# Down projection, output blocks 0 to 7: all 22 k pairs by seven products in two passes, and the FFN norm's factor moved onto the up projection's input

## The chip, the cores and the metric

One Trainium2 chip, one of its cores. The metric is device time in microseconds of one execution of the whole kernel. Engines are named as in the profile: PE is TensorE's matmuls, PEld its weight loads, DVE is VectorE, ACT ScalarE, POOL GpSimd, SP the engine that issues most DMAs.

## The reference

One layer of a bidirectional encoder with 256 tokens and 2048 channels in float32: a mixer (attention and a state space branch), then a gated feed-forward part with a convolution over tokens, then a final RMSNorm. The change touches the feed-forward part:

```python
def conv_ffn(h, w_up, conv_w, conv_b, w_down):
    u = centred_dwconv(h @ w_up, conv_w, conv_b)
    gate, val = jnp.split(u, 2, axis=-1)
    return (jax.nn.silu(gate) * val) @ w_down
...
    h = h + conv_ffn(rms_norm(h, norm_ffn_w[l]), ffn_w_up[l], ffn_conv_w[l], ffn_conv_b[l],
                     ffn_w_down[l])
return rms_norm(h, norm_final_w)
```

`w_up` has 2048 rows and 2 x 5632 columns, `w_down` 5632 rows and 2048 columns, and the convolution takes three tokens. In blocks of 128: 16 channel blocks, 44 gate and 44 value blocks, 16 output blocks.

## The kernel before, in words

**Numbers in two parts.** Every float32 operand of a product is split into a high part (a copy on ScalarE into a rounded type, `wh`) and a low part (what is left, a subtraction on VectorE, `wl`), by `hilo` (L149) or in `split_to` (L205). A product is three matmuls: high by high, high by low, low by high. Weights come in by DMA on SP's queue into three raw buffers (`RAWB=3`, `load`, L119) and are split in halves of eight 128x128 blocks into five buffers for each part (`HB=5`), so splits run up to five halves ahead of TensorE, and a raw buffer is loaded again once the job in it is split.

**Jobs.** The program is a list of jobs, each with a weight source, a function that issues its matmuls by half, an evacuation, and side functions (`at`, L1309) that run just ahead of it. A `dense` job (L235) multiplies 16 (or 14) blocks of weights with the activations. Its high parts go first (L252, one matmul of 512 columns per block, which gives high and low of the input side by side), then its low parts (L259, one of 256). Jobs marked `mate` go by twos: high of both, then low of both (main loop, L1589 on). With `late` set, the last so many blocks of both high parts are put behind the rest (`high`, L1552).

**Up projection.** For each of 44 up pairs m there is one gate and one value job. Their input is `hHL`, the residual stream times the norm's weight, made by `wo_evac` (L1066) before the norm's factor r_ffn is known; `ffn_r` (L1082) makes r_ffn at the end of the first up job. `conv3` (L1088) therefore multiplies the job's result by r_ffn (`sum_times`, L304: a copy on ScalarE, an addition in L302 and a multiplication in L309 on VectorE), then convolves (L1091, L1093). `gate_ev` and `val_ev` make the activation `aHL[kp]`, where k pair kp holds the blocks 2kp and 2kp+1.

**Down projection, output blocks 0 to 7.** Eight output blocks and one k pair make a 2x2 product of block matrices: two halves of 128 tokens by two k blocks, and two k blocks by two groups of four output blocks. Products of 128 tokens with 512 columns accumulate in PSUM over the k pairs. For k pairs 0 to 17 (`sevens`, L1122) it is done with seven products in place of eight, from sums of activations (`act_sums`, L1124, names W1, R, N4, N2) and sums of weights. Four of the seven (M1, M5, M7, M6) are the first pass, `unit_one` (L1152), which runs between up pairs: one behind every even m from 2 to 36. It splits the raw weights B11 and three sums of weights (`split_one`, L178), and stores three things in DRAM for later: the sum T2 (`t2D`), the activation sum N4 (`n4D`), and for kp below 14 the activation itself (`aD`). The other three (M2, M3, M4) are the second pass, `second` (L1170, `split_two` L195), which loads two quarters of the weights, T2, and by `n4_load` and `a_load` N4 and the activation. Three second units stand behind up pairs 38, 40 and 42; the rest come after the up projection. k pairs 18 to 21 are `plain` (L1183): eight products into M2, M3, M4 and a fourth sum P22. `inner` (L1194) takes the first four sums out of PSUM when k pair 17 is done, `last_unit` (L1205) the other four when all is done; `seven_channels` (L1219) turns the result back to channels during block 12.

**Output blocks 8 to 15** are dense jobs: `d8` to `d15` for k blocks 28 to 43, and `e8` to `e15` for k blocks 0 to 27, whose activations `a_load` brings back. The order after the up projection is written by hand in L1482 to L1484 (`p` plain, `s` second, `d` and `e` as above), and by which job each reload is put ahead of (L1480, L1499).

**Buffers and order.** Activations, sums and reloads share 29 page buffers; TensorE's sums use eight PSUM banks, four for dense jobs and four for M1 to M7 and small things. Engines take their instructions in order; that order is made ahead of time from the program's order and dependencies. SP issues the loads, the stores and the reloads from one queue.

## Time and profile before

| what | us |
|---|---|
| runs before | 1935.64, 1936.91, 1933.70 (median 1935.64) |
| the profiled execution | 1935.64 |
| its span | 1933.1 |
| TensorE busy | 1919.3 |
| VectorE busy | 1610.6 |
| ScalarE busy | 1274.1 |
| up projection, with the down units in it | about 1197 to 1744 |
| rest of the down projection | about 1744 to 1920 |

The page of the profile gives the busy time of each engine and the costliest groups of instructions; a group's row reads: line, engine, operation, output <- inputs with shapes, count, then busy time and mean duration, then the engine's idle time just ahead of them and what ended it. Matmul durations there overlap, so that a matmul's price is read from how many follow each other in a stretch.

### The profile page before, as it was taken

Reading aid. Unit: us, or ns where it says so; the run is one execution under the profiler, and the core shown is the slowest. Engines: PE = TensorE matmul, PEld = TensorE weight load, DVE = VectorE, ACT = ScalarE, POOL = GpSimd, SP = SyncE. Lnnn points to the kernel's source line nnn. Section 1 sums busy time; section 2 is a strip of 40 time slices with the busy share of each in tenths; the row PEclk is TensorE's granted clock in tenths of the full one; section 3 lists DMA queues with packets and bytes.
Section 4 is the critical chain, followed back from the end, with each engine's and each line's share of the span. In section 5 each row is a group of like instructions: output and inputs, shape, how many; then the busy total and the mean of one; then the engine's idle time right before and its main releaser. Section 6 shows DMA issues by size and latency. Waiting matters only on the chain.

```text
span 1933.1 us, 28910 instructions
## 1 busy us (share of the span) xinstructions
PE 1919.3 (99%) x10812; PEld 1678.0 (87%) x10812; DVE 1610.6 (83%) x2690; ACT 1274.1 (66%) x2048; POOL 16.2 (1%) x36
## 2 busy tenths in 40 slices
...
GB/s 284 207 155 145 170 131 229 275 220 173 218 223 172 216 231 169 211 239 162 173 196 202 216 250 175 228 254 245 255 239 237 250 243 229 227 214 337 272 261 112
DMA packets 170859, 417.82 MB, mean 216 GB/s; under 512 B 10720, under 2 KB 108192, under 8 KB 143840
## 3 DMA queue, kind: packets, MB, share of 16 engines
...
q0 software_dynamic: 1024, 1.54, 0.3%
...
## 4 chain that ended last, share of the span: by engine, by line
PE 92%; DVE 3%; ACT 2%; DMA 2%; issue 1%; SPq 0%; DVEq 0%; ACTq 0%
PE g L252 36%; PE g L259 19%; PE g L977 11%; PE s L1143 5%; PE g L287 3%; PE g L288 3%; PE g L289 3%; PE s L977 2%; PE g L231 1%; PE g L233 1%; PE g L232 1%; DVE wl L226 1%; PE s L252 1%; PE s L882 1%; PE s L891 1%
## 5 line engine op out<-in xcount | busy, mean ns | idle before, releaser
L226 DVE TENSOR_TENSOR wl<-raw,wh 128x1024 fp32r<-128x1024 f32 x598 | 716.0, 1212 | 164.9 <-ACT wh L225 89.6
L225 ACT ACTIVATE wh<-raw 128x1024 fp32r<-128x1024 f32 x598 | 620.2, 1049 | 275.3 <-PE g L252 80.7
L252 PE MATMUL g<-xHL,wh 128*128 128x512 f32 x1424 | 341.7, 392 | 0.2 <-DVE cu L302 0.2
L252 PE MATMUL g<-hHL,wh 128*128 128x512 f32 x1408 | 327.2, 390 | 0.0
L252 PEld LDWEIGHTS g<-hHL,wh 128*128 128x128 f32 x1408 | 262.8, 188 | 53.5
L252 PEld LDWEIGHTS g<-xHL,wh 128*128 128x128 f32 x1424 | 262.5, 188 | 52.1 <-PE s L233 0.4
L259 PEld LDWEIGHTS g<-xHL,wl 128*128 128x128 f32 x1424 | 182.6, 191 | 6.9
L259 PE MATMUL g<-xHL,wl 128*128 128x256 f32 x1424 | 184.7, 283 | 0.0
L259 PEld LDWEIGHTS g<-hHL,wl 128*128 128x128 f32 x1408 | 174.8, 192 | 3.4
L259 PE MATMUL g<-hHL,wl 128*128 128x256 f32 x1408 | 176.0, 283 | 0.0
L150 ACT ACTIVATE wh<-raw 128x1024 fp32r<-128x1024 f32 (+1 forms) x118 | 87.0, 752 | 83.6 <-DMA raw<-in_w_dn 30.3
L977 PE MATMUL g<-wh,yHL 128*128 128x512 f32 x392 | 125.0, 390 | 0.0
L151 DVE TENSOR_TENSOR wl<-raw,wh 128x1024 fp32r<-128x1024 f32 (+1 forms) x118 | 96.6, 839 | 11.2 <-PE g L259 5.9
L1093 DVE SCALAR_TENSOR_TENSOR uc<-u,V,uc 128x255 f32<-128x255 f32 x176 | 84.3, 479 | 20.6 <-ACT uc L1091 18.4
L287 PE MATMUL g<-wh,xHL 128*128 128x512 f32 x256 | 100.4, 392 | 0.0
L288 PE MATMUL g<-wl,xHL 128*128 128x512 f32 x256 | 100.0, 390 | 0.0
L289 PE MATMUL g<-wh,xHL 128*128 128x512 f32 x256 | 99.8, 390 | 0.0
L1091 ACT ACTIVATE uc<-u,V 128x256 f32<-128x256 f32 x88 | 52.0, 591 | 62.3 <-DVE u L309 62.3
L977 PEld LDWEIGHTS g<-wh,yHL 128*128 128x128 f32 x392 | 73.6, 188 | 15.2
L252 PE MATMUL g<-aHL,wh 128*128 128x512 f32 x338 | 78.9, 390 | 0.0
L977 PE MATMUL g<-wl,yHL 128*128 128x512 f32 x196 | 76.3, 389 | 0.0
L252 PEld LDWEIGHTS g<-aHL,wh 128*128 128x128 f32 x338 | 63.2, 188 | 13.1
...
## 6 DMA issues: line engine op xcount, KB each, us to landing
...
raw<-in_w_in SPq DMA_DIRECT2D x128, 256.0 KB, 3.9
...
FB<-acsD SPq DMA_DIRECT2D x32, 512.0 KB, 7.3
...
```

The source lines that it names most:

```text
L150: act.activation(wh, v, AF.Copy)
L151: dve.tensor_sub(wl, v, f32(wh))
L225: act.activation(vh, r, AF.Copy)
L226: dve.tensor_sub(vl, r, f32(vh))
L252: pe.matmul(ps, lhsT=wh[:, b, :], rhs=x, start=k == 0, stop=False)
L259: pe.matmul(cell["ps"][:, 0, :], lhsT=wl[:, b, :], rhs=get(k)[:, 0, :], start=False, stop=k == ktot - 1)
L287: pe.matmul(ps, lhsT=x[:, 0, ts], rhs=wH[:, kk, :], start=k == 0, stop=False)
L288: pe.matmul(ps, lhsT=x[:, 0, ts], rhs=wL[:, kk, :], start=False, stop=False)
L289: pe.matmul(ps, lhsT=x[:, 1, ts], rhs=wH[:, kk, :], start=False, stop=k == kt - 1)
L977: pe.matmul(M[nm], lhsT=x, rhs=w, start=left[nm] == total[nm], stop=left[nm] == 1)
L1093: dve.scalar_tensor_tensor(o[:, a], u[:, b], vcol("fcw", k * 88 + cb), o[:, a], ALU.mult, ALU.add)
L1143: pe.matmul(M[nm], lhsT=x, rhs=w, start=left[nm] == total[nm], stop=left[nm] == 1)
```

## The change

- The sets of products change. First pass: M5, M7, M6, M4, from the sums W1, R, N2 and the activation A22 and from four sums of weights (T13 with two, T24 with two), so that `split_one` makes four sums and splits two halves of 1024 columns. Second pass: M1, M2 and M3 from three of the four weight quarters as loaded, without a sum: `split_two` has no addition, and its source is 512 KB and 256 KB of `w_dn`. T2 is no longer stored or loaded.
- All 22 k pairs go this way; `plain` and P22 are gone. `inner` works on M5, M6, M7, M4 when the last first unit is done, `last_unit` on M1, M2, M3.
- First units 0 to 20 stand behind up pairs 5, 7, 9, 11, 13, 15, 17, 18, 20, 22, 24, 26, 28, 30, 31, 33, 35, 37, 39, 41 and 42; unit 21 behind `d9`. No second unit stands in the up projection. The order after it begins with `d8 d9`, and `d8` has `late = 2`.
- `rescale` makes the input again with the factor in it: for each of the eight pairs of channel blocks two operations of VectorE (residual times weight times r_ffn), a high and a low, put ahead of jobs of up pairs 1 to 5. From up pair 6 on the jobs read it, and `conv3` no longer multiplies.
- N4 is reloaded in six groups at other places, activations from `u21` on.

```diff
@@ -132,7 +132,7 @@
             for h in range(2):
                 nc.sync.dma_start(t[:, 8 * h:8 * h + 8, :], j.src[:, 8 * h:8 * h + 8, :])
         elif j.seven == 2:
-            nc.sync.dma_start(t[:, :8, :], j.src[0])
+            nc.sync.dma_start(t[:, :8, :].rearrange("p (m k) c -> p m (k c)", m=4), j.src[0])
             nc.sync.dma_start(t[:, 8:12, :], j.src[1])
         elif j.wide:
             nc.sync.dma_start(t.rearrange("p (m k) c -> p m (k c)", m=8), j.src)
@@ -179,28 +179,23 @@
 
 
         r = raws[i].rearrange("p (m k) c -> p m k c", m=8)
-        B11, B12, B22 = r[:, :4, 0, :], r[:, 4:, 0, :], r[:, 4:, 1, :]
+        B11, B12, B21, B22 = r[:, :4, 0, :], r[:, 4:, 0, :], r[:, :4, 1, :], r[:, 4:, 1, :]
         if h == 0:
-            t, t2 = page([P, 2, 4, P], name="T13"), page([P, 4, P], name="T2")
-            sums[i], T2[jobs[i].kp] = t, t2
+            t, u = sums[i] = page([P, 2, 4, P], name="T13"), page([P, 2, 4, P], name="T24")
             dve.tensor_add(t[:, 0], B11, B12)
             dve.tensor_add(t[:, 1], B22, B12)
-            hilo(wh[:, :4, :], wl[:, :4, :], B11)
-            hilo(wh[:, 4:, :], wl[:, 4:, :], t[:, 0])
-            dve.tensor_add(t2, t[:, 0], B22)
+            hilo(wh, wl, t.rearrange("p t m c -> p (t m) c"))
+            dve.tensor_add(u[:, 0], t[:, 0], B22)
+            dve.tensor_add(u[:, 1], u[:, 0], B21)
         else:
-            hilo(wh[:, :4, :], wl[:, :4, :], sums.pop(i)[:, 1])
-            hilo(wh[:, 4:, :], wl[:, 4:, :], T2[jobs[i].kp])
+            hilo(wh, wl, sums.pop(i)[1].rearrange("p t m c -> p (t m) c"))
 
     def split_two(i, h, wh, wl):
-        r = raws[i]
         if h == 0:
-            dve.tensor_add(r[:, 8:12, :], r[:, 8:12, :], r[:, 0:4, :])
-            hilo(wh, wl, r[:, 0:8, :])
+            vh, vl = (w.rearrange("p (k m) c -> p m k c", k=2) for w in (wh, wl))
+            hilo(vh, vl, raws[i][:, :8, :].rearrange("p (m k) c -> p m k c", m=4))
         else:
-            hilo(wh[:, :4, :], wl[:, :4, :], r[:, 8:12, :])
-
-    T2 = {}
+            hilo(wh[:, :4, :], wl[:, :4, :], raws[i][:, 8:12, :])
 
     def split_to(n):
         while hptr[0] < min(n, len(halves)):
@@ -300,13 +295,6 @@
     def halves_sum(ps, o):
         act.activation(o, ps[:, 1, :], AF.Copy)
         dve.tensor_add(o, o, ps[:, 0, :])
-
-    def sum_times(ps, r, o):
-        if len(ps.shape) == 2:
-            dve.tensor_mul(o, ps, r)
-        else:
-            halves_sum(ps, o)
-            dve.tensor_mul(o, o, r)
 
     def token_sums(accs):
 
@@ -1083,11 +1071,25 @@
         r_ffn["r"] = rsqrt_of([ssh], D, "r_ffn")
 
 
+    TURNED = 6
+    nF = {}
+
+    def rescale(j):
+        v = page([P, 2, S], name="nF")
+        t = nF[j] = page([P, 2, 2, S], F32R, name="hHL")
+        for b in range(2):
+            m = 2 * j + b
+            dve.scalar_tensor_tensor(v[:, b, :], hp[m // 4][:, m % 4, :], vcol("nffn", m), r_ffn["r"], ALU.mult,
+                                     ALU.mult)
+        hilo(t[:, 0], t[:, 1], v)
+
     gv, aHL = {}, {}
 
     def conv3(ps, cb):
         u, o = p1(name="u"), p1(name="uc")
-        sum_times(ps, r_ffn["r"], u)
+        halves_sum(ps, u)
+        if cb % NFF < TURNED:
+            dve.tensor_mul(u, u, r_ffn["r"])
         act.activation(o, u, AF.Identity, scale=vcol("fcw", 88 + cb), bias=vcol("fcb", cb))
         for k, a, b in ((0, slice(1, S), slice(0, S - 1)), (2, slice(0, S - 1), slice(1, S))):
             dve.scalar_tensor_tensor(o[:, a], u[:, b], vcol("fcw", k * 88 + cb), o[:, a], ALU.mult, ALU.add)
@@ -1111,15 +1113,14 @@
             dve.tensor_sub(lo, o, f32(hi))
             if m % 2 == 0:
                 even[0] = o
-            elif m // 2 in sevens:
+            else:
                 act_sums(aS, m // 2, even[0], o)
         return ev
 
 
 
     even, aS = {}, {}
-    NS, NK = 18, 22
-    sevens = set(range(NS))
+    NK = 22
 
     def act_sums(st, kp, e, o):
         w = page([P, 4, P], name="asum")
@@ -1130,17 +1131,15 @@
 
     aD = dr.tile([NK, P, 2, 2, S], F32, name="aD")
     n4D = dr.tile([NK, P, 2, P], F32, name="n4D")
-    t2D = dr.tile([NK, P, 4, P], F32, name="t2D")
     n4, M, tok, left = {}, {}, {}, {}
-    for nm in ("M1", "M5", "M7", "M6", "M2", "M3", "M4", "P22"):
-        left[nm] = (3 * NS if nm != "P22" else 0) + (6 * (NK - NS) if nm in ("M2", "M3", "M4", "P22") else 0)
-    total = dict(left)
+    for nm in ("M5", "M7", "M6", "M4", "M1", "M2", "M3"):
+        left[nm] = 3 * NK
 
     def add(nm, aH, aL, bH, bL):
         if nm not in M:
             M[nm] = spsum([P, 512])
         for x, w in ((aH, bH), (aH, bL), (aL, bH)):
-            pe.matmul(M[nm], lhsT=x, rhs=w, start=left[nm] == total[nm], stop=left[nm] == 1)
+            pe.matmul(M[nm], lhsT=x, rhs=w, start=left[nm] == 3 * NK, stop=left[nm] == 1)
             left[nm] -= 1
 
     def half(w, a):
@@ -1151,62 +1150,54 @@
 
     def unit_one(kp, spill):
         def mm(h, n, wh, wl):
-            for a, (nm, lf) in enumerate(((("M1", "A11"), ("M5", "W1")), (("M7", "R"), ("M6", "N2")))[h]):
+            for a, (nm, lf) in enumerate(((("M5", "W1"), ("M7", "R")), (("M6", "N2"), ("M4", "A22")))[h]):
                 add(nm, *seven_left(aHL[kp], aS[kp], lf), half(wh, a), half(wl, a))
             if h == 1:
-                nc.sync.dma_start(t2D[kp], T2.pop(kp))
                 for i in range(2):
                     nc.sync.dma_start(n4D[kp, :, i, :], f32(aS[kp][i][:, 2, :]))
                 if spill:
                     nc.sync.dma_start(aD[kp], f32(aHL[kp]))
 
         def ev():
-            if kp == NS - 1:
+            if kp == NK - 1:
                 inner()
         j = Job(dn_src(kp), 16, mm, ev)
-        j.wide, j.seven, j.kp = True, 1, kp
+        j.wide, j.seven = True, 1
         jobs.append(j)
 
     def second(kp):
         def mm(h, n, wh, wl):
-            o = [aHL[kp][:, i, 1, :] for i in range(2)]
             if h == 0:
-                add("M2", o[0][:, :P], o[1][:, :P], half(wh, 0), half(wl, 0))
-                add("M3", n4[kp // 4][:, kp % 4, 0, :], n4[kp // 4][:, kp % 4, 1, :], half(wh, 1), half(wl, 1))
+                for k, nm in ((0, "M1"), (1, "M2")):
+                    add(nm, *(aHL[kp][:, i, k, :P] for i in range(2)), half(wh, k), half(wl, k))
             else:
-                add("M4", o[0][:, P:], o[1][:, P:], half(wh, 0), half(wl, 0))
-        k1 = 2 * kp + 1
-        j = Job((w_dn[0:8, :, k1 * P:k1 * P + P].rearrange("m p c -> p m c"), t2D[kp]), 16, mm, last_unit)
+                add("M3", *(n4[kp // 4][:, kp % 4, i, :] for i in range(2)), half(wh, 0), half(wl, 0))
+        k = slice(2 * kp * P, 2 * kp * P + 2 * P)
+        j = Job((w_dn[0:4, :, k].rearrange("m p c -> p m c"),
+                 w_dn[4:8, :, k.start + P:k.stop].rearrange("m p c -> p m c")), 16, mm, last_unit)
         j.seven = 2
         jobs.append(j)
 
-    def plain(kp):
-        def mm(h, n, wh, wl):
-            wH, wL = (w.rearrange("p (k m) c -> p k (m c)", k=2) for w in (wh, wl))
-            for k in range(2):
-                for t, nm in ((0, ("M2", "M3")[h]), (1, ("M4", "P22")[h])):
-                    aH, aL = (aHL[kp][:, j, k, t * P:(t + 1) * P] for j in range(2))
-                    add(nm, aH, aL, wH[:, k, :], wL[:, k, :])
-        j = Job(dn_src(kp), 16, mm, last_unit)
-        j.wide = True
-        jobs.append(j)
-
     def inner():
-        c, v = page([P, 2, 512], name="m15"), page([P, 2, 512], name="vx")
-        m1, m5, V, X = c[:, 0, :], c[:, 1, :], v[:, 0, :], v[:, 1, :]
-        act.activation(m1, M.pop("M1"), AF.Copy)
+        c, v = page([P, 2, 512], name="m65"), page([P, 2, 512], name="vx")
+        m6, m5, X, Y = c[:, 0, :], c[:, 1, :], v[:, 0, :], v[:, 1, :]
         act.activation(m5, M.pop("M5"), AF.Copy)
-        dve.tensor_sub(V, M.pop("M6"), m1)
-        dve.tensor_add(X, M.pop("M7"), V)
-        dve.tensor_add(V, V, m5)
+        act.activation(m6, M.pop("M6"), AF.Copy)
+        dve.tensor_add(X, M.pop("M7"), m6)
+        dve.tensor_add(Y, m6, m5)
         dve.tensor_add(m5, X, m5)
-        tok.update({(0, 0): m1, (1, 0): X, (0, 1): V, (1, 1): m5})
+        dve.tensor_sub(X, M.pop("M4"), X)
+        tok.update({(0, 0): m6, (1, 0): X, (0, 1): Y, (1, 1): m5})
 
     def last_unit():
         if any(left.values()):
             return
-        for nm, o in (("M2", tok[0, 0]), ("M4", tok[1, 0]), ("M3", tok[0, 1]), ("P22", tok[1, 1])):
-            dve.tensor_tensor(o, M.pop(nm), o, ALU.subtract if nm == "M4" else ALU.add)
+        m1 = page([P, 512], name="m1")
+        act.activation(m1, M.pop("M1"), AF.Copy)
+        dve.tensor_add(tok[0, 1], M.pop("M3"), tok[0, 1])
+        dve.tensor_add(tok[0, 0], M.pop("M2"), m1)
+        for c, op in (((1, 0), ALU.add), ((0, 1), ALU.subtract), ((1, 1), ALU.subtract)):
+            dve.tensor_tensor(tok[c], tok[c], m1, op)
 
     def n4_load(g, n):
         n4[g] = page([P, 4, 2, P], F32R, name="n4")
@@ -1468,20 +1459,20 @@
     b = len(jobs)
     turns = [b]
     K0 = 14
+    first = {5 + (37 * kp + 19) // 20: kp for kp in range(21)}
+    assert len(first) == 21 and all(2 * kp + 2 <= m < NFF for m, kp in first.items())
+    slots = []
     for m in range(NFF):
+        slots.append(len(jobs))
         dense(w_up[2 * m], 16, lambda k: pair(hHL, k), gate_ev(m)).mate = True
         dense(w_up[2 * m + 1], 16, lambda k: pair(hHL, k), val_ev(m))
-        kp = m // 2 - 1
-        if m % 2 == 0 and 0 <= kp < NS:
-            unit_one(kp, kp < K0)
-        elif m % 2 == 0 and kp >= NS:
-            second(K0 + kp - NS)
-    e = len(jobs)
-    for g, i in ((3, -16), (4, -9), (0, 7), (1, 13), (2, 18)):
-        at(e + i, n4_load, g, 4 if g < 4 else NS - 16)
-    plain(18)
-    second(17)
-    seq = "d8 d9 p19 p20 d10 d11 p21 s0 d12 d13 s1 s2 s3 d14 d15 s4 s5 e8 s6 s7 e9 s8 s9 e10 s10 s11 e11 s12 s13 e12 e13 e14 e15"
+        if m in first:
+            unit_one(first[m], first[m] < K0)
+    for j, (p, o) in enumerate(((1, 0), (1, 1), (2, 0), (2, 1), (3, 1), (4, 0), (4, 1), (5, 0))):
+        at(slots[p] + o, rescale, j)
+    at(slots[TURNED], hHL.update, nF)
+    seq = ("d8 d9 u21 d10 d11 s14 s15 d12 d13 s16 s17 d14 d15 s18 s19 s20 s21 s0 e8 s1 s2 s3 e9 s4 s5 s6 e10 s7 s8 s9 "
+           "e11 s10 s11 s12 s13 e12 e13 e14 e15")
     lo = {}
     for w in seq.split():
         i, n = len(jobs), int(w[1:])
@@ -1495,15 +1486,19 @@
         elif w[0] == "e":
             down_last(n, 2 * K0)
         else:
-            (plain if w[0] == "p" else second)(n)
+            unit_one(n, False) if w[0] == "u" else second(n)
+    turns.append(lo["d8"])
+    for g, w in enumerate("s20 e8 s5 d8 d10 s16".split()):
+        at(lo[w], n4_load, g, min(4, NK - 4 * g))
     for kp in range(K0):
-        at(lo["p19"] + kp if kp < 11 else lo["s4"] + kp - 11, a_load, kp)
+        at(lo["u21"] + kp if kp < 11 else lo["s18"] + kp - 11, a_load, kp)
     for i in range(4):
         at(lo["e12"] + 1 + i, seven_channels, i)
     jobs[b].post.append(ffn_r)
 
     for i in turns:
         jobs[i].late = 1
+    jobs[lo["d8"]].late = 2
 
 
     assert all(i in gate_blocks for i in range(win_i[0], w_in.shape[0])) and gs[0] == ga[0] == 16
```

## The prediction

> **What bounds the kernel now.** I read the page first, then busy time by stretch, then TensorE's waits, then the chain that ended last.
>
> ```profile
> span 1933.1 us, 28910 instructions
> PE 1919.3 (99%) x10812; PEld 1678.0 (87%) x10812; DVE 1610.6 (83%) x2690; ACT 1274.1 (66%) x2048; POOL 16.2 (1%) x36
> ```
>
> Of a span of 1933.1 us TensorE is idle for 13.8. The profiled execution took 1935.64 us, which is also the median of the runs before, so 2.5 us lie around the span and sums can be made against either. The change touches the up projection and what follows it. Busy time by stretch there (PE, PEld, DVE, ACT, POOL, then granted clock, share of the DMA engines, GB/s), a stretch of the up projection without a down unit, one with six, and the second pass from block 8 to the last pair:
>
> ```profile
> 1209.00:1220.60 11.60, 11.60 (x71) 10.32 (x70) 8.23 (x17) 7.99 (x13) 0.00 (x0) 1.00 0.53 180
> 1234.62:1384.30 149.68, 149.68 (x841) 131.63 (x841) 136.45 (x240) 93.28 (x151) 0.00 (x0) 1.00 0.71 247
> 1751.84:1880.08 128.24, 128.24 (x679) 110.99 (x679) 86.65 (x110) 64.44 (x77) 0.00 (x0) 1.00 0.85 285
> ```
>
> TensorE is busy in all of it at the full granted clock. VectorE is second, at 91% beside the units, and DMA second in the second pass, at 85%. TensorE's waits from the up projection's start to the last job of the down projection are one row (total, times, longest):
>
> ```profile
> PE s L1143 <- DVE wl L151: 1.1, 2, 0.6
> ```
>
> So whatever is no product can give back 1.1 us at most; the rest has to come out of the products. Their price is in the chain that ended last (start, us, what):
>
> ```profile
> 1256.82 2.75 PE s L1143 x12
> 1259.57 7.25 PE g L252 x32
> 1266.82 3.83 PE g L259 x32
> ...
> 1803.51 6.15 PE s L1143 x27
> 1809.66 7.25 PE g L252 x32
> ```
>
> Twelve down products follow each other every 2.75 / 12 = 0.229 us; an up pair (gate and value job of one block) is 7.25 + 3.83 = 11.08 us; a first-pass unit is 12 products, 2.75 us, a second-pass unit 9, 6.15 / 3 = 2.05 us.
>
> **Part 1, the products.** A k pair in two passes costs seven products of three matmuls, 21; a plain pair eight of three, 24. Four plain k pairs become seven-product pairs: 12 matmuls fewer, 12 x 0.229 = 2.75 us, all on TensorE, which sets the end. This is the one term that nothing hides.
>
> The Trainium skill, TensorE: Matmul & The Clock Gate, Back-to-back issue gap, gives a stream of loads and matmuls at 512 columns about 131 ns each; an estimate by that page is a gain of 12 x 0.131 = 1.57 us. The chain above has 229 ns, so the trace does not bear that figure out for this kernel's matmuls.
>
> **Part 2, VectorE from the seventh up pair on.** Groups by shape in the stretch with six units (count, then busy us and mean ns, then idle before):
>
> ```profile
> L226 DVE TENSOR_TENSOR wl<-raw,wh 128x1024 fp32r<-128x1024 f32 x48 | 57.5, 1217 | 1.7 <-PE g L259 1.7
> L225 ACT ACTIVATE wh<-raw 128x1024 fp32r<-128x1024 f32 x48 | 49.8, 1052 | 11.9 <-DMA raw<-in_w_up 11.0
> L1093 DVE SCALAR_TENSOR_TENSOR uc<-u,V,uc 128x255 f32<-128x255 f32 x48 | 23.0, 479 | 5.6 <-ACT uc L1091 4.9
> L151 DVE TENSOR_TENSOR wl<-T,wh 128x512 fp32r<-128x512 f32 x18 | 12.3, 681 | 0.0
> L309 DVE TENSOR_TENSOR u<-u,r_ffn 128x256 f32<-128x256 f32 x24 | 10.0, 416 | 0.0
> L186 DVE TENSOR_TENSOR T<-raw 128x512 f32<-128x512 f32 x6 | 4.1, 683 | 0.0
> L937 DVE TENSOR_TENSOR asum<-uc 128x128 f32<-128x128 f32 x6 | 1.8, 293 | 0.2
> ```
>
> Of the 88 multiplications in L309, 76 go: 76 x 0.416 = 31.6 us of VectorE. They are not on the path: the window has TensorE busy throughout. A unit's split has two lows of 1024 instead of four of 512 (2 x 1.217 - 4 x 0.681 = -0.29) and four sums instead of three (+0.68). Per two up pairs and one unit, 24.91 us of TensorE, VectorE loses 4 x 0.416 - 0.39 = 1.27 us of 136.45 / 6 = 22.7. Units come at 20 in 37 up pairs instead of one in two, which takes about half a microsecond of that back; VectorE ends near 88%. The two waits on L151 happened where it was late; I take them as gone, -1.1 us, with 0 as the other end. With every other unit, four more stores of n4 to DRAM are issued and none of T2; SP waits in that queue less, not more.
>
> **Part 3, the rescale in up pairs 1 to 5.** Each of its eight steps adds two products with a column and a row (nearest row L1093, 0.479), one copy on ScalarE, and one low of 512 (0.681): 1.64 us of VectorE, 13.1 in all. No unit stands now until behind up pair 5, but the multiplications stay until then and sums for three k pairs fall here (3 x (4 x 0.293 + 0.681) = 5.6), then unit 0's split (4 x 0.683 + 2 x 1.217 = 5.2). Five up pairs of 8.23 us (first window above) are 41.2. Together 65.1; successive VectorE instructions overlap by about 0.07 us (busy time of the window against the sum of its groups: 240 instructions, about 150 against 136), so some 62. TensorE takes 5 x 11.08 + 2.75 = 58.2. VectorE falls about 4 us behind by unit 0. What hides it: the second half of unit 0 gets its buffer when the first of the four low halves of up pair 5 is through, 3/4 x 3.83 = 2.87 us ahead of the unit, and TensorE needs its low at the unit's eighth matmul, 7 x 0.229 = 1.6 us into it; less the low's own 1.22 us, 3.3 us may be lost. 4 against 3.3: I take +1.0 us, between 0 (ScalarE's turn-around hidden, the lag never built up) and 4.
>
> **Part 4, the join with block 8.** Plain pair 18 and second-pass pair 17 no longer stand between the last up pair and block 8; the last two k of blocks 8 and 9 are put behind the rest. Block 8 and 9 then have 28 matmuls, 28 x 7.25 / 32 = 6.3 us, and one more, before they read the last activation. VectorE's rows after an odd up pair whose low ended at 1266.82 + 3.83 = 1270.65:
>
> ```profile
> 1276.93 0.42 DVE L1111 TENSOR_TENSOR aHL<-uc,aHL 128x256 fp32r<-128x256 f32 x1
> 1277.26 0.28 DVE L939 TENSOR_TENSOR asum<-uc,asum 128x128 f32<-128x128 f32 x1
> 1277.46 0.68 DVE L186 TENSOR_TENSOR T<-raw 128x512 f32<-128x512 f32 x1
> ```
>
> The activation is there 6.7 us after the low's end, 6.3 without the multiplication: cost 0, at most 0.5 if that chain is queued behind block 9's splits. The end of the second pass has one copy and one 128x512 operation more; block 12's first 28 matmuls, 6.3 us, and their lows lie before the first reader. Cost 0; uncovered it would be two operations of that size, about 2 x 0.68 = 1.4.
>
> **Part 5, the loads of the second pass.** SP's issues of weight loads around a run of three second-pass units that TensorE ran from 1803.51, and the DMA view of the whole pass (count, KB, us to landing):
>
> ```profile
> 1785.80 0.38 SPq L135 DMA_DIRECT2D raw<-in_w_dn  x1
> ...
> 1795.20 0.38 SPq L135 DMA_DIRECT2D raw<-in_w_dn  x1
> ...
> 1801.46 3.02 SPq L144 DMA_DIRECT2D raw<-in_w_dn  x2
> ```
>
> ```profile
> DMA packets 24340, 36.80 MB, mean 285 GB/s; under 512 B 972, under 2 KB 18991, under 8 KB 23563
> ...
> raw<-in_w_dn SPq DMA_DIRECT2D x14, 512.0 KB, 5.1
> aHL<-aD SPq DMA_DIRECT2D x11, 512.0 KB, 6.9
> raw<-t2D SPq DMA_DIRECT2D x14, 256.0 KB, 5.3
> n<-n4D SPq DMA_DIRECT2D x3, 512.0 KB, 7.1
> ```
>
> 285 GB/s at a share of 0.85 means about 335 GB/s at full. From block 8 to the last pair the pass gains eight second-pass units of 0.786 MB, one first-pass unit of 1.05 and 1.31 of n4, and loses three plain pairs of 1.05: 42.3 MB, 126 us at 335. TensorE's side is 128.24 + 8 x 2.05 - 3 x 5.5 + 2.75 = 131 us. On average it still fits, at 96%. It does not fit in place: units 18 to 21 and 0 now stand in one run with three activation loads and one n4 load, 5 x 0.786 + 4 x 0.524 = 6.0 MB, 18.0 us, against 5 x 2.05 = 10.3. The 7.7 us must be brought ahead. In before the first load of a run was issued 17.7 us ahead of its unit, the third 1807.61 - 1795.20 = 12.4, and the job behind the run 1809.66 - 1801.46 = 8.2. A load is issued once the raw buffer of three jobs earlier is split, and splits go five halves ahead; by that, in a run of five, the fourth, the fifth and the job behind it have about 8 us each. They need 5.1 to 6.9 to land, 1.05 for the high and, in a unit, 1.22 for the low: 7.4 to 9.2. I take +1.0 us, between 0 and 7.7. The new unit's split has no sum to form and its first half waits for one load of two, which is why I stay near the lower end.
>
> The Trainium skill, DMA: Bandwidth & Descriptors, Where 436 GB/s comes from, puts the HBM limit of one core at about 358 GB/s; an estimate by that page is 42.3 / 0.358 = 118 us. The share row here gives 335 and binds earlier, though neither is over 131.
>
> **Sum.** -2.75 - 1.1 + 1.0 + 0 + 1.0 = -1.85: 1935.64 - 1.85 = 1933.8 us. A measurement of this kernel can tell about 0.2%, 3.9 us, from no change: the forecast is "no change".
>
> **Rivals.** *All is covered*: lag and loads stay hidden and the L151 waits go: 1935.64 - 3.85 = 1931.8. For it speaks that TensorE waited nowhere in the second pass at 85%; against it that two places are pressed beyond anything in before. *The load queue takes over at block 8's first 28 k (the job behind unit 0)*: if the landing there comes later than 10.3 us after unit 18 starts, TensorE waits for it, up to 7.7 us, 1939.5, and with the run of four behind block 11 about 1941. For it: 18 us of loads against 10.3. Against it: 17.7 us of lead at a run's head. *Units behind an even up pair become a chain*: both halves of a unit now start from sums; the first half of before started from the raw weights. VectorE late by ScalarE's wait for a raw buffer, and the unit behind the rows of part 4:
>
> ```profile
> 1443.42 0.42 DVE L1111 TENSOR_TENSOR aHL<-uc,aHL 128x256 fp32r<-128x256 f32 x1 [2.32 <-ACT aHL L1110]
> ```
>
> ```profile
> 1281.77 2.75 PE s L1143 x12
> ```
>
> The first sum ran at 1277.46; two sums, a copy of 1.05 and a low of 1.22 end at 1281.1, 0.7 us ahead of the unit's start. Late by 2.3 us, with 0.8 less in front (two multiplications), each of eight such units (behind up pairs 18 to 30, and 42) would wait 0.8 us: 1931.8 + 6.4 = 1938.2. Against it: before was that late only in one stretch. *The freed VectorE time is worth something*: it can't be over 1.1, since there are no other waits.
>
> **How the numbers follow.** Forecast 0.46 (its own range 1932 to 1937), all covered 0.26, load queue 0.16, chain 0.07, something unseen 0.05. Faster by over 0.2% (below 1931.8): half of "all covered", 0.13, and 0.07 of the forecast's own lower end. Slower (above 1939.5): 0.12 of the load queue, 0.02 of the chain where it meets other waits, 0.04 of the unseen: 0.18. Within: 0.62. The range from 1930.8 to 1940.5 takes in the first rival with the scatter of a run and most of the slower two.
>
> **What would show it.** Right: 12 matmuls fewer, TensorE's waits in the up projection at most 1 us in place of L151's two, a wait of about a microsecond at the first unit, behind up pair 5, one at the first job of block 8's first 28 k or at units 21 and 0; L309 gone from up pair 6 on and VectorE near 88% there. Wrong: waits of TensorE on DMA landings that add up to over 4 us in the second pass, a wait on L151 or its copy at each of eight units, or a span below 1929.

## The result, and the profile after

The kernel after takes 1943.74 us (median of 6 runs, 1942.54 to 1947.06) against 1936.22 before (6 runs in the same comparison): a ratio of 1.0043, 95% interval 1.003 to 1.0056. It is slower by 7.5 us, where 1933.8 and "no change" were forecast, and it lies above the range. The profiled execution took 1943.82 us.

The page after, its first line and the busy times:

```profile
span 1942.0 us, 28865 instructions
PE 1921.0 (99%) x10800; PEld 1677.4 (86%) x10800; DVE 1616.6 (83%) x2647; ACT 1281.4 (66%) x2033; POOL 16.2 (1%) x36
```

The span grew by 8.9. TensorE has its 12 matmuls fewer and is busy 1.7 us more: a matmul on a slow clock counts as busy, so busy time alone does not show what was lost. TensorE's waits from the start of the up projection to the last job of the down projection (total, times, longest):

```profile
PE s L1142 <- ACT wh L150: 3.8, 3, 2.7
PE g L247 <- ACT wh L220: 2.6, 1, 2.6
PE s L1142 <- DVE wl L151: 0.8, 2, 0.5
```

Where before had two waits of 1.1 us in sum, there are six now, of 7.2. They stand at two places.

**Unit 0, behind up pair 5.** Windows of after (stretch, its length, then busy us of PE, PEld, DVE, ACT, POOL, then granted clock, DMA share, GB/s): up pair 3, unit 0, and the rest of the up projection:

```profile
1232.60:1243.70 11.10, 11.10 (x65) 9.83 (x65) 11.10 (x21) 6.92 (x12) 0.00 (x0) 1.00 0.72 249
1268.60:1275.00 6.40, 6.06 (x13) 4.30 (x14) 6.40 (x10) 5.60 (x7) 0.00 (x0) 0.50 0.49 164
1297.29:1734.10 436.81, 436.81 (x2439) 383.63 (x2438) 387.19 (x620) 268.08 (x403) 0.00 (x0) 1.00 0.66 232
```

VectorE is busy every moment of up pair 3; in the stretch to 1734 it is at 387.19 / 436.81 = 89% and TensorE waits nowhere. At unit 0 the granted clock is 0.50; by the trace's record of the clock it stands there from 1268.4 to 1275.2. The unit's matmuls on TensorE, the copies on ScalarE that they wait for, and VectorE's work ahead of those (start, us, what, idle before and its releaser):

```profile
1268.63 1.22 PE L1142 MATMUL s<-wh,aS 128*128 128x512 f32 x2 [2.69 <-ACT wh L150]
1270.16 0.79 PE L1142 MATMUL s<-wh,aS 128*128 128x512 f32 x1 [0.31 <-ACT wh L150]
...
1271.18 0.63 PE L1142 MATMUL s<-wh,aS 128*128 128x512 f32 x1
1271.61 0.63 PE L1142 MATMUL s<-wl,aS 128*128 128x512 f32 x1
```

```profile
1267.52 1.06 ACT L150 ACTIVATE wh<-T 128x1024 fp32r<-128x1024 f32 x1 [1.51 <-DVE T L186]
```

```profile
1264.47 0.88 DVE L1082 SCALAR_TENSOR_TENSOR nF<-h,V,r_ffn 128x256 f32<-128x256 f32 x2
1265.26 0.42 DVE L1113 TENSOR_TENSOR aHL<-uc,aHL 128x256 fp32r<-128x256 f32 x1
1265.60 0.68 DVE L185 TENSOR_TENSOR T<-raw 128x512 f32<-128x512 f32 x1
1266.20 0.68 DVE L151 TENSOR_TENSOR hHL<-nF,hHL 128x512 fp32r<-128x512 f32 x1
1266.80 0.68 DVE L186 TENSOR_TENSOR T<-raw 128x512 f32<-128x512 f32 x1
```

The first sum of weights begins at 1265.60, with the multiplications of the last rescale step ahead of it and that step's low (L151, hHL) between it and the second sum; the copy of both ends at 1268.58, and TensorE, done with up pair 5 at 1265.9, waits 2.69 us for it. Then its matmuls follow each other every 0.43 us instead of 0.229. So the place costs 3.0 us of waiting and, for 13 matmuls (the count in the window), 13 x 0.20 = 2.6 of slow clock.

**The end of the run of five second units.** In the chain that ended last, the load of block 8's first 14 k and what follows it:

```profile
1812.48 9.16 DMA raw<-in_w_dn
1822.86 6.65 PE g L247 x28
```

Before, the chain ran from there to the end of the down projection through TensorE alone; at the same job:

```profile
1820.74 4.11 PE s L1143 x18
1824.85 6.35 PE g L252 x28
```

Two stretches of 10 us around it, after:

```profile
1810.00:1820.00 10.00, 8.32 (x33) 5.45 (x31) 5.21 (x6) 3.38 (x5) 0.00 (x0) 1.00 1.08 376
1820.00:1830.00 10.00, 7.38 (x36) 6.02 (x35) 5.33 (x5) 5.72 (x7) 0.00 (x0) 1.00 0.99 320
```

and the DMA view of 1770 to 1825 (count, KB, us to landing):

```profile
DMA packets 12703, 20.70 MB, mean 376 GB/s; under 512 B 610, under 2 KB 10267, under 8 KB 12187
...
aHL<-aD SPq DMA_DIRECT2D x10, 512.0 KB, 8.7
raw<-in_w_dn SPq DMA_DIRECT2D x9, 512.0 KB, 6.7
```

The same window before:

```profile
DMA packets 10535, 16.22 MB, mean 295 GB/s; under 512 B 448, under 2 KB 7972, under 8 KB 10020
...
aHL<-aD SPq DMA_DIRECT2D x8, 512.0 KB, 6.6
raw<-in_w_dn SPq DMA_DIRECT2D x7, 512.0 KB, 5.5
```

Now the queue is full, and transfers of the same size (512 KB of weights, an activation) that landed in 5.5 and 6.6 us take 6.7 and 8.7. TensorE has four waits here: 0.24 at unit 21, 0.81 and 0.53 at unit 0, and 2.62 at block 8.

**The balance.** The length of the up projection (first of its matmuls to the end of the last) and of the rest (to the last down matmul), by the trace:

| kernel | up projection | rest |
|---|---|---|
| before | 546.9 | 176.6 |
| after, by products and L151's waits alone | 547.9 | 171.7 |
| after, measured | 553.6 | 177.7 |

The second row: 21 units of 2.75 in place of 18 and three of 2.05 are +2.1 in the up projection, the waits -1.1; the rest has -2.75 - 2.1. Over that row lie 5.7 us in the up projection and 6.0 in the rest; ahead of the up projection and behind the last matmul another 1.1. -3.85 + 5.7 + 6.0 + 1.1 is the 8.9 of the span.

### The profile page after: what moved, and what is told of

It reads as the page before. It is cut to its first block, busy times and chain, and to the rows that moved or that the text cites. A ratio compares the mean times of both kernels' runs of the same rounds, so it can differ in the third digit from the quotient of the medians.

```text
span 1942.0 us, 28865 instructions
## 1 busy us (share of the span) xinstructions
PE 1921.0 (99%) x10800; PEld 1677.4 (86%) x10800; DVE 1616.6 (83%) x2647; ACT 1281.4 (66%) x2033; POOL 16.2 (1%) x36
## 3 DMA queue, kind: packets, MB, share of 16 engines
q0 software_dynamic: 1024, 1.54, 0.3%
q10 hardware_dynamic: 768, 1.09, 0.2%
## 4 chain that ended last, share of the span: by engine, by line
PE 91%; DVE 5%; DMA 2%; ACT 1%; issue 0%; SPq 0%; DVEq 0%; ACTq 0%
PE g L247 36%; PE g L254 19%; PE g L965 9%; PE s L1142 5%; PE g L282 3%; PE g L283 3%; PE g L284 3%; PE s L965 2%; DVE wl L221 2%; PE g L226 1%; PE g L228 1%; PE g L227 1%; DMA raw<-in_w_os 1%; PE s L247 1%; PE s L870 1%; PE s L879 1%
## 5 line engine op out<-in xcount | busy, mean ns | idle before, releaser
L221 DVE TENSOR_TENSOR wl<-raw,wh 128x1024 fp32r<-128x1024 f32 x590 | 707.5, 1213 | 178.9 <-ACT wh L220 98.1
L220 ACT ACTIVATE wh<-raw 128x1024 fp32r<-128x1024 f32 x590 | 609.1, 1048 | 248.0 <-PE g L247 83.1
L254 PEld LDWEIGHTS g<-xHL,wl 128*128 128x128 f32 x1424 | 182.6, 191 | 6.9
L254 PE MATMUL g<-xHL,wl 128*128 128x256 f32 x1424 | 184.8, 283 | 0.0
L254 PEld LDWEIGHTS g<-hHL,wl 128*128 128x128 f32 x1408 | 174.8, 192 | 3.4
L254 PE MATMUL g<-hHL,wl 128*128 128x256 f32 x1408 | 176.1, 283 | 0.0
L150 ACT ACTIVATE wh<-raw 128x1024 fp32r<-128x1024 f32 (+1 forms) x108 | 81.0, 777 | 67.2 <-DMA raw<-in_w_dn 19.6
L151 DVE TENSOR_TENSOR wl<-raw,wh 128x1024 fp32r<-128x1024 f32 (+1 forms) x108 | 91.5, 875 | 25.1 <-ACT wh L150 13.7
L150 ACT ACTIVATE wh<-T 128x1024 fp32r<-128x1024 f32 x60 | 63.7, 1061 | 57.8 <-DVE T L189 22.8
L151 DVE TENSOR_TENSOR wl<-T,wh 128x1024 fp32r<-128x1024 f32 x60 | 73.4, 1223 | 15.5 <-ACT wh L150 11.9
```

Source lines behind the costliest of these rows:

```text
L150: act.activation(wh, v, AF.Copy)
L151: dve.tensor_sub(wl, v, f32(wh))
L220: act.activation(vh, r, AF.Copy)
L221: dve.tensor_sub(vl, r, f32(vh))
L254: pe.matmul(cell["ps"][:, 0, :], lhsT=wl[:, b, :], rhs=get(k)[:, 0, :], start=False, stop=k == ktot - 1)
```

## The experiments

Theory after the result: (A) VectorE is overloaded in up pairs 2 to 4 by the rescale, unit 0 comes late, and the gap lets TensorE's clock fall; (B) the DMA queue is full ahead of block 8's first 28 k. Each run below is a change of the kernel after, unless it says otherwise; the lengths of its up projection and rest stand in the table at the end of this section. A run's figures in brackets are its ratio to before and the 95% interval of that.

**Without the rescale** (the multiplication by the factor stays everywhere):

```diff
-    TURNED = 6
+    TURNED = 44
-    for j, (p, o) in enumerate(...): at(slots[p] + o, rescale, j)
-    at(slots[TURNED], hHL.update, nF)
```

> The changed kernel without the rescale: every up job is multiplied by the norm's factor after the product, as in before. Theory (VectorE is overfull in up pairs 1 to 5, so unit 0 waits, and the wait halves TensorE's clock): the first unit behind up pair 5 no longer waits and its 12 matmuls take 2.75 us; 6.6 us come back, less up to 1.5 for waits on lows later, so 1937 to 1939. Rival (unit 0 is late because both of its halves now start from sums): the wait of about 3 us at unit 0 stays, and the time is 1943 to 1945.

1945.47 us (1.0052, 1.004 to 1.0065): missed, and the rival's wait is not there either. The wait at unit 0 is gone, but the up projection is only 1 us shorter. Its waits on lows there, and its windows from 1420 on:

```profile
PE s L1142 <- DVE wl L151: 1.8, 3, 0.8
```

```profile
1420.00:1480.00 60.00, 58.72 (x328) 50.71 (x327) 55.24 (x96) 33.74 (x52) 0.00 (x0) 1.00 0.69 241
1480.00:1740.00 260.00, 258.89 (x1438) 225.05 (x1437) 241.96 (x404) 158.38 (x238) 0.00 (x0) 1.00 0.66 222
```

VectorE is at 92 to 93% and TensorE loses its time in small pieces at units behind even up pairs, 1431.58 the first. The up projection still loses 4.7 us, so the rescale is worth some 5 us to this kernel's units; what it costs is where it was put.

**The gap at unit 0 filled** with 12 matmuls of 512 columns into an unused bank, on data that is there:

```diff
+            if m == 5:
+                at(len(jobs), fill)
```

> The changed kernel with 12 matmuls of 512 columns into an unused bank ahead of unit 0, in the place where TensorE waits 2.7 us. Nothing that the output needs changes. Theory (the half clock at unit 0 comes from the idle time ahead of it): the fill takes the idle time's place, the granted clock stays full, unit 0 takes 2.75 us instead of 6, and the time falls by 3 us to about 1940.5. Rival (the slow matmuls there have another cause, such as late operands): nothing is gained or up to 2.7 us is lost, 1943.5 to 1946.5.

1942.71 us (1.0037, 1.0025 to 1.005), between the two expectations; the profiled execution took 1941.08. The fill is 2.75 us on TensorE, and one wait is left in the whole up projection:

```profile
PE s L1142 <- ACT wh L150: 0.8, 1, 0.8
```

The granted clock is 1.00 in both windows of 10 us there, and the up projection is 2.3 us shorter with 2.75 us of work more. So the half clock at this place comes from the gap. The Trainium skill, TensorE: Matmul & The Clock Gate, Why this matters for your kernels, advises against idle gaps over about 3 us; here one of 2.69 was enough.

**Units one pair later**:

```diff
-    first = {5 + (37 * kp + 19) // 20: kp for kp in range(21)}
+    first = {6 + (36 * kp + 18) // 20: kp for kp in range(21)}
```

> The changed kernel with the first units one up pair later: unit kp behind up pair 6 + (36 kp + 18) // 20, so unit 0 behind 6, the last still behind 42. Theory (VectorE's backlog from up pairs 1 to 5): up pair 6 has no multiplication and no rescale, VectorE wins some 2 us back, and the wait at unit 0 falls below 1.5 us, short enough to keep the clock: -5 to -6.6, 1937 to 1939. Rival (the wait belongs to the first unit wherever it stands): same time as the changed kernel within 1.5 us.

1940.78 us (1.0031, 1.0019 to 1.0044), between the two expectations. Units 0 and 1 wait four times about 0.5 us and the clock stays up there: the up projection loses 2.5 in place of 5.7. VectorE's lag is paid off with time.

**The rescale alone, put on the kernel before**, with its multiplications from up pair 6 on gone and nothing else changed:

```diff
-        sum_times(ps, r_ffn["r"], u)
+        halves_sum(ps, u)
+        if cb % NFF < TURNED:
+            dve.tensor_mul(u, u, r_ffn["r"])
```

> The kernel before with nothing but the rescale added: eight steps ahead of up pairs 1 to 5, no multiplication from up pair 6 on; products, units and order as before. Theory (VectorE is overfull in up pairs 1 to 5): units 0 and 1 stand behind pairs 2 and 4 here, VectorE has some 62 to 64 us of work for 61 of TensorE, so up to 3 us are lost there and before's 1.7 us at k pairs 10 and 11 come back: between -1 and +2 us against before. Rival (the rescale by itself gains what it takes off VectorE): -1.7 or more, nothing lost in up pairs 1 to 5.

1939.74 us (1.002, 1.0011 to 1.0029; 11 runs): 3.6 us over before, where the theory's upper end was 2. Units 0 and 1 stand behind up pairs 2 and 4 there:

```profile
1233.56 0.50 PE L1157 MATMUL s<-wh,aS 128*128 128x512 f32 x1 [0.56 <-ACT wh L150]
1234.71 0.50 PE L1157 MATMUL s<-wl,aS 128*128 128x512 f32 x1 [0.64 <-DVE wl L151]
1263.02 0.50 PE L1157 MATMUL s<-wh,aS 128*128 128x512 f32 x1 [1.38 <-ACT wh L150]
```

```profile
1236.00:1239.30 3.30, 3.30 (x9) 2.62 (x9) 3.30 (x7) 3.30 (x7) 0.00 (x0) 0.50 0.63 166
```

The last line is part of why the size was missed: behind the gaps of 0.56 and 0.64 the granted clock is 0.50 for 3.4 us, so a half clock follows gaps much shorter than that of 2.69 too. Only the up projection is longer (551.7 against 546.9); the rest stays at 176.6. So the rescale brings the first loss by itself; the second does not come from it, but with the new sets of products and their order.

**The rescale spread**, one step in each of up pairs 1 to 8, units from pair 8 on:

```diff
-    TURNED = 6
+    TURNED = 9
-    first = {5 + (37 * kp + 19) // 20: kp for kp in range(21)}
+    first = {8 + (34 * kp + 17) // 20: kp for kp in range(21)}
-    ... ((1, 0), (1, 1), (2, 0), (2, 1), (3, 1), (4, 0), (4, 1), (5, 0))
+    ... ((1, 1), (2, 1), (3, 1), (4, 1), (5, 1), (6, 1), (7, 1), (8, 1))
```

> One rescale step per up pair, in pairs 1 to 8, the new input read from pair 9 on, units from pair 8 on. VectorE then has 8.2 + 1.6 = 9.9 us of 11.1 in each of these pairs and can't fall behind. Theory (the loss at unit 0 is VectorE's overload in pairs 2 to 4, doubled by the half clock after the gap): the up projection loses at most 1 us of its 6.4, so 1943.7 - 5.6 = 1938.1, between 1936.5 and 1939.5, tail unchanged. Rival (the units' longer split chain behind even up pairs costs its own, and shows wherever VectorE has no slack, as it did spread over the last pairs in the run without the rescale): 21 units in 35 pairs in place of 38 bring waits behind even pairs late in the up projection, 3 to 5 us of them, 1940.5 to 1942.5.

1940.83 us (1.0026, 1.0018 to 1.0035; 11 runs): above the theory's range and within the rival's. The place decides between them. The up projection loses 1.7 in place of 5.7, all of it at one place:

```profile
1297.00:1312.00 15.00, 13.40 (x68) 10.61 (x67) 14.86 (x23) 10.68 (x15) 0.00 (x0) 1.00 0.59 199
1312.00:1740.00 428.00, 428.00 (x2397) 376.02 (x2395) 382.87 (x611) 264.03 (x397) 0.00 (x0) 1.00 0.68 233
```

The theory holds for the up projection, 0.7 short of its bound of 1: unit 0 stands behind an even up pair (8) now, and VectorE is at 14.86 of 15.00 us around it. The rival's waits late in the up projection are not there: with 21 units in 35 pairs TensorE waits nowhere from 1312 to its end. The 4.0 us gained against the kernel after would give 1939.7; the rest is 1.4 longer in the profiled execution (see behind the table).

**The second pass in runs of three**:

```diff
-  d10 d11 s14 s15 d12 d13 s16 s17 d14 d15 s18 s19 s20 s21 s0 e8
+  d10 d11 s14 s15 s16 d12 d13 s17 s18 s19 d14 d15 s20 s21 s0 e8
```

> The changed kernel with the same second-pass units ahead of block 8's first 28 k, but in runs of three between the block pairs instead of two, two and five, and the last three activation reloads put ahead of unit 20 on. Theory A (the lead of a load shrinks in a run of five): the wait at the first job of block 8's first 28 k goes, -5, about 1939. Theory B (the queue is full from block 10 on, whatever the order, since the same bytes have to land ahead of that job): the waits move but their sum stays within 1.5 us of the changed kernel, 1942 to 1945.

1942.47 us (1.0037, 1.0023 to 1.0051), within theory B's range. The waits spread (1.7 us ahead of block 14, 0.5 at block 8, 0.2 at each of two units), the rest is 0.8 shorter. It was read as a full queue, whatever the order; that reading was narrowed later.

**Unit 0 behind block 8's first 28 k**, N4's reloads there too:

```diff
-    s20 s21 s0 e8 s1 s2 s3 e9 ... "s20 e8 s5 d8 d10 s16"
+    s20 s21 e8 s0 s1 s2 s3 e9 ... "e8 e9 e10 d8 d10 s16"
```

> The changed kernel with second-pass unit 0 and the n4 reloads moved behind block 8's first 28 k: 1.31 MB less have to land ahead of that job, 2.06 us less of TensorE's work lie ahead of it. Theory B: the loss there falls from 5.7 us by 1.31 / 0.37 = 3.5 less the 2.06 us that TensorE arrives earlier, so by about 1.5 and by more where the clock no longer halves: 1940 to 1942.5. Theory A (run length): the run is four instead of five, the wait goes, 1938 to 1939.

1941.09 us (1.0031, 1.0019 to 1.0042): as theory B expected, the rest 2.0 shorter. Block 8 still waits, 1.4 us.

**Reloads of activations earlier**:

```diff
-        at(lo["u21"] + kp if kp < 11 else lo["s18"] + kp - 11, a_load, kp)
+        at(lo["d8"] + kp if kp < 11 else lo["d14"] + kp - 11, a_load, kp)
```

> The changed kernel with each activation reload put two to four jobs earlier, from block 8 on instead of from the last first unit on; same bytes, same order of work. Theory B: the queue's free time from block 8 to 10 (share 0.6 to 0.85 there) takes up to 1 MB, 2.8 us, of what now falls into the full stretch, so the loss of 5.7 falls to 3 or less: 1940.5 to 1941.5. Theory A: the reloads are not in the way, the time stays, 1943 to 1945.

1944.82 us (1.0048, 1.0034 to 1.0062): no gain, as theory A has it, but for another reason. The row of SP's waits from 1780 to 1830 that matters (total, times, longest) and the moved GB/s in the 40 slices of 1770 to 1825 (the line of the DMA view):

```profile
SPq L1208 <- PE g L254: 7.4, 2, 7.1
```

```profile
GB/s 304 410 438 429 417 417 414 390 346 348 371 350 368 428 387 387 448 396 404 360 339 371 348 187 13 39 337 353 343 371 355 322 330 327 420 415 407 352 346 315
```

A reload (L1208) needs a page, and the next page comes free only when block 15's lows (L254) have read the activation in it. SP waits 7.1 us at it, the weight loads stand behind it, and the queue falls to 13 GB/s.

**Two activations kept in their pages** instead of reloaded (k pairs 12 and 13):

```diff
-            unit_one(first[m], first[m] < K0)
+            unit_one(first[m], first[m] < 12)
-    for kp in range(K0):
+    for kp in range(12):
```

> Activations of k pairs 12 and 13 stay in their pages and are not reloaded: 2 x 0.524 = 1.05 MB less ahead of block 8's first 28 k, at 376 GB/s 2.8 us. Theory (full queue): the loss in the tail falls from 5.7 to about 2.9, 1943.7 - 2.8 = 1940.9, between 1940 and 1942. Rival (pages): two pages fewer in the second half of the up projection bring new waits there and for the reloads, 1943 or more.

1945.06 us (1.0045, 1.0031 to 1.0058): the rival's case, by the same wait (6.7 us at one reload). The pages, not the bytes, say when the last reloads can start.

**Fewer bytes, the same instructions otherwise**:

```diff
+        if kp in (18, 19, 20, 21, 0):
+            j.src = j.src[:1]
```

> Leaves out the 256 KB load of the second pass's third weight quarter for k pairs 18 to 21 and 0 (M3 then takes the quarter that is there, so part of the output is computed from other weights); the instructions of TensorE, VectorE and ScalarE are the same. 5 x 0.262 = 1.31 MB less, at 376 GB/s 3.5 us. Theory (the DMA queue is full from 1770 to 1825 and everything must land ahead of block 8's first 28 k): the loss behind unit 18 falls from 5.7 to about 2, 1943.7 - 3.5 = 1940.2, between 1939 and 1941.3. Rival (the wait is set by when raw buffers come free and how far ahead splits go, not by bytes): at most 1 us less, 1942.7 to 1943.7.

1942.49 us (1.0031, 1.0019 to 1.0042): nearer to the rival. The most telling trace of all: TensorE waits nowhere in units 18 to 21 and 0 now (1.6 us after), the copies of the last of them wait for TensorE instead of DMA, and block 8 waits all the same. SP's issue of its first load, ScalarE's copies of unit 0 and of that load, and TensorE:

```profile
1811.39 0.34 SPq L145 DMA_DIRECT2D raw<-in_w_dn  x1
```

```profile
1813.31 1.58 ACT L151 ACTIVATE wh<-raw 128x1024 fp32r<-128x1024 f32 x2 [2.14 <-PE s L1144]
1819.31 1.79 ACT L222 ACTIVATE wh<-raw 128x1024 fp32r<-128x1024 f32 x2 [4.42 <-DMA raw<-in_w_dn]
```

```profile
1820.42 8.26 PE L249 MATMUL g<-aHL,wh 128*128 128x512 f32 x28 [3.10 <-ACT wh L222]
```

The load is issued when the raw buffer of unit 20 is split, and that follows TensorE; it lands 7.8 us later. The lead is fixed by the buffers and the wait is lead against landing. The 28 matmuls take 8.26 us in place of 6.65 because the granted clock is 0.50 for 3.4 us of them, so the time gained at the units is mostly lost here again. In SP's queue, here as after, N4's reload and the last activation's, 0.5 MB each, stand just ahead of it.

**These two reloads behind that load** (same order of TensorE's work):

```diff
-    "s20 e8 s5 d8 d10 s16"; at(... else lo["s18"] + kp - 11, a_load, kp)
+    "s21 e8 s5 d8 d10 s16"; at(... else lo[("s18", "s19", "s0")[kp - 11]], a_load, kp)
```

> Order of TensorE's work as in the change; only the last activation's reload and N4's for unit 0 move from ahead of unit 20 to behind the issue of block 8's first weight load. Theory now (lead against landing: that load can be issued only when unit 20 is split, some 8 us before its use, and lands in 8 to 9 us because two reloads of 0.5 MB stand just ahead of it in a full queue): its landing falls by about 2 us, the wait of 2.6 at block 8 to under 1, and the tail's loss from 5.7 to 3 to 4, so 1941 to 1942. Rival (the queue is simply full, whatever stands where): the wait moves to the reloaded activation or stays, 1943 to 1944.

1942.3 us (1.0036, 1.0022 to 1.0049). The wait is as expected; the rest is 4.7 over its sum where 3 to 4 were expected, and the median's gain of 1.4 is no larger than the intervals. So the order's effect on the wait is shown, its effect on the time by itself is not. The issue of the load, its copy, and TensorE's wait at block 8:

```profile
1810.11 0.34 SPq L144 DMA_DIRECT2D raw<-in_w_dn  x1
```

```profile
1817.38 1.79 ACT L220 ACTIVATE wh<-raw 128x1024 fp32r<-128x1024 f32 x2 [1.52 <-DMA raw<-in_w_dn]
```

```profile
PE g L247 <- ACT wh L220: 0.6, 1, 0.6
```

The load lands 7.2 us after its issue instead of 9.16, the wait is 0.6 instead of 2.6. The waits at units 21 and 0 stay (1.5 us in three).

**That and the spread rescale, units from pair 9 on**:

```diff
-    first = {5 + (37 * kp + 19) // 20: kp for kp in range(21)}
+    first = {9 + (33 * kp + 16) // 20: kp for kp in range(21)}
```

> The reloads of the run before this one, with the rescale spread over pairs 1 to 8 and units from pair 9 on, which stands behind an odd pair. The two losses are independent by the theory: the up projection's falls from 6.4 to at most 1, the tail's by about 2: 1943.7 - 5.4 - 2 = 1936.3, between 1935 and 1938. Rival (units closer together bring their own waits, as the 2.4 left in the run with the spread rescale): 1938 to 1940.

1937.05 us (1.0004, 0.9995 to 1.0013; 11 runs): as expected, but not all for the reason given. The up projection takes 547.7 and TensorE waits nowhere in it, which is the 5.4 forecast and a little more. The rest was forecast 2 us shorter and is 177.9 in the profiled execution, as after: block 8 waits only 0.4, the units ahead of it 2.4.

**With unit 0 behind block 8's first 28 k as well**, and the last two activations behind both of its first loads:

```diff
-    s20 s21 s0 e8 s1 s2 s3 e9 ... lo["s18"] + kp - 11
+    s20 s21 e8 s0 s1 s2 s3 e9 ... lo[("s19", "s21", "s21")[kp - 11]]
```

> Unit 0 behind block 8's first 28 k as in the run with that order, and the last two activations' reloads behind the issue of block 8's first two loads; rescale spread, units from pair 9 on. Theory (lead against landing): tail's loss 2 or less, up projection's 1 or less: 1943.7 - 5.4 - 3.7 = 1934.6, between 1933.5 and 1937. Rival (full queue whatever the order): tail still 4, 1937 to 1939.

1935.27 us (0.9996, 0.9987 to 1.0006; 11 runs), within what was expected for the time; the rest loses 3.4, where the theory had 2 or less and the rival 4. Three stretches of its tail:

```profile
1790.00:1800.00 10.00, 10.00 (x56) 8.69 (x56) 6.25 (x8) 4.70 (x6) 0.00 (x0) 1.00 1.07 361
1800.00:1810.00 10.00, 9.50 (x47) 7.72 (x46) 6.14 (x8) 4.14 (x6) 0.00 (x0) 1.00 1.02 329
1810.00:1820.00 10.00, 9.39 (x53) 8.27 (x54) 6.02 (x6) 4.67 (x6) 0.00 (x0) 1.00 1.07 355
```

The share of the DMA engines is as high as in the kernel after (0.99 to 1.09 in the stretches of 10 us from 1770 to 1830), and TensorE loses 0.5 and 0.6 us where it lost 1.7 and 2.6. Block 8's first load, issued 4.6 us behind the nearest reload and not half a microsecond behind two, lands in 5.1 us where it took 9.16: for that load a full queue is not the loss, what stands just ahead of it is. It is issued only 5.5 us before TensorE could use it, and its copy takes 1.1, so 1.1 us of wait stay. Block 8's second load then stands in the chain that ended last: its landing, copies and lows let the load of the third unit behind block 8 be issued, and TensorE waits 0.3 and 0.2 us there:

```profile
1805.73 6.27 DMA raw<-in_w_dn
...
1816.12 7.21 DMA raw<-in_w_dn
```

This suggests that the three raw buffers set the pace there; no run has a fourth.

**The same in runs of three, three and two**:

```diff
-    s14 s15 d12 d13 s16 s17 d14 d15 s18 s19 s20 s21 s0 e8 ... lo["s18"] + kp - 11
+    s14 s15 s16 d12 d13 s17 s18 s19 d14 d15 s20 s21 e8 s0 ... lo[("s20", "s20", "s21")[kp - 11]]
```

> As the one before, with the second pass in runs of three, three and two ahead of block 8's first 28 k in place of two, two and four, and the last three reloads around the issue of block 8's first loads. Theory: the run ahead of it is two units, so fewer loads compete: tail's loss 0 to 2, 1933 to 1936. Rival (full queue): 1937 to 1939; or the last reload itself lands late for block 8's last blocks, then a wait there of 1 to 3 us.

1936.25 us (1.0001, 0.9992 to 1.001; 11 runs): between the two expectations. It waits 0.9 and 1.7 us ahead of two dense blocks, 1777.7 and 1797.0, and not at block 8.

**All three ideas of before the order was understood** (spread rescale, two activations kept, unit 0 behind):

> The rescale spread over pairs 1 to 8, two activations kept, and unit 0 and N4's reloads behind block 8's first 28 k (as in the run with that order). If the two losses are independent and both theories hold: 1943.7 - 5.6 (up projection) - 2.8 (bytes) - 1.9 (order) = 1933.4, between 1932 and 1936; that would be 2 to 3 us faster than before. If the up projection's new waits come with the closer units: 1936 to 1938. If pages run short: 1938 or more.

1939.55 us (1.0018, 1.0009 to 1.0027): the last of the three cases, with SP's wait for a page (7.4 us) in it.

**More bytes**, two copies of 0.5 MB from DRAM to DRAM meant for units 18 and 19:

```diff
+    for i, w in enumerate(("s18", "s19")):
+        at(lo[w], more, i)
```

> The changed kernel with two copies of 0.52 MB from DRAM to DRAM added at second-pass units 18 and 19, read by nothing. Theory B (the queue is full ahead of block 8's first 28 k): 1.05 MB at about 370 GB/s push that job back by 2.8 us, 1946 to 1947. Theory A (only the lead of single loads counts, the queue has room): less than 1 us, 1943 to 1945.

1960.6 us (1.013, 1.0116 to 1.0144). The copies were not held back to those units: SP issued them at 1312 and 1418 us, inside the up projection, where TensorE waited 4.58 us at one place and 5.48 at another. It says nothing on the tail.

Lengths in the profiled executions; what lies over 547.9 and 171.7 is lost (the rescale on before has before's products and does not go by these sums). The column of half clock is the time at a granted clock of 0.50, in us, in the up projection and in the rest, by the trace's record of the clock:

| kernel | up projection | rest | at half clock | median | ratio |
|---|---|---|---|---|---|
| after | 553.6 | 177.7 | 6.8, 0 | 1943.74 | 1.0043 |
| without the rescale | 552.6 | 180.4 | 0, 3.4 | 1945.47 | 1.0052 |
| gap filled (2.75 of fill) | 551.3 | 178.5 | 0, 0 | 1942.71 | 1.0037 |
| units one pair later | 550.4 | 180.9 | 0, 3.4 | 1940.78 | 1.0031 |
| rescale on before | 551.7 | 176.6 | 3.4, 0 | 1939.74 | 1.002 |
| rescale spread | 549.6 | 179.1 | 0, 3.4 | 1940.83 | 1.0026 |
| runs of three | 552.8 | 176.9 | 3.4, 0 | 1942.47 | 1.0037 |
| unit 0 behind | 552.8 | 175.7 | 3.4, 0 | 1941.09 | 1.0031 |
| reloads earlier | 553.4 | 178.3 | 3.4, 0 | 1944.82 | 1.0048 |
| two kept | 553.4 | 179.4 | 6.8, 3.4 | 1945.06 | 1.0045 |
| fewer bytes | 553.4 | 177.0 | 6.8, 3.4 | 1942.49 | 1.0031 |
| reloads behind the load | 552.9 | 176.4 | 3.4, 0 | 1942.3 | 1.0036 |
| and rescale spread | 547.7 | 177.9 | 0, 0 | 1937.05 | 1.0004 |
| and unit 0 behind | 547.9 | 175.1 | 0, 0 | 1935.27 | 0.9996 |
| in runs of three and two | 547.7 | 176.5 | 0, 0 | 1936.25 | 1.0001 |
| all three ideas | 549.6 | 177.7 | 0, 3.4 | 1939.55 | 1.0018 |
| more bytes | 569.1 | 179.8 | 17.1, 3.4 | 1960.6 | 1.013 |

The rest varies from one profiled execution to another where its order is the same (177.7 to 180.9: after, without the rescale, gap filled, units later, rescale spread). In three of these five, block 8's wait of 2.67 or 2.68 us ends in 3.4 us of half clock, as here in the run with the rescale spread:

```profile
1818.10:1821.40 3.30, 2.85 (x7) 2.30 (x8) 2.65 (x3) 2.77 (x4) 0.00 (x0) 0.50 1.02 305
```

In the other two it is 2.62 and 2.63, and the clock stays at 1.00. So one profiled execution is no measure of the rest, and the medians carry the verdicts there.

## Why the prediction was wrong, point by point

- **Part 1** (12 matmuls, -2.75) was right: TensorE has 10800 matmuls instead of 10812, and in the three kernels that mend both losses ("and rescale spread" to "in runs of three and two" in the table) the up projection is within 0.2 us of the sum of products and waits.
- **Part 2** (VectorE near 88% from the seventh pair on, the L151 waits gone) was right: 89%, and no wait there. "It can't be over 1.1, since there are no other waits" was wrong as a price: without the rescale the new units lose 4.7 us. VectorE's time is worth what the changed kernel would wait without it, not what the old one waited. The rival of a chain behind even up pairs is that same loss; the rescale keeps it away.
- **Part 3 failed** at "4 against 3.3: I take +1.0 us". The lag was foreseen, the cover was not looked at in the right place: 3.3 us were figured for the low of the unit's second half, while the high of its first half, a sum of weights and a copy, is needed by the first matmul, and the first sum stood behind the rescale. The wait is 3.0. The wait alone lies within the bounds of 0 to 4. Outside them is the other 2.6, the half clock that the gap brings: a term that the sum did not have, since the price was of waiting alone and no row that the prediction rests on showed a half clock. 5.7 in place of 1.0.
- **Part 4** (the join with block 8, 0) was right: no wait there.
- **Part 5 failed** at "I stay near the lower end". Place and mechanism were right, the job behind unit 0 with some 8 us of lead against its landing; the landing (5.1 to 6.9) was taken from a queue that had slack. In the new queue it was 9.16. "335 at full" was too low as well (376 measured over 55 us), so the rate was not what failed. Of the four waits, the 1.6 us at units 21 and 0 went with 1.31 MB less to load; the 2.6 at block 8 did not, it went with the order of the loads. (The 376 lie above the limit of about 358 GB/s that the Trainium skill, DMA: Bandwidth & Descriptors, Where 436 GB/s comes from, gives; the measurement decides.) 6.0 in place of 1.0, within the 0 to 7.7.
- **The range**: the two losses were taken as cases beside each other. They stand in different stages and add up: their upper ends of 4 and 7.7 on 1935.64 - 3.85 give 1943.5, and the range stopped at 1940.5. That this meets the measured 1943.74 is chance: the losses were 5.7, 6.0 and 1.1 elsewhere.

Shown by runs: that the first loss comes from the rescale's place and goes with its spreading; that the clock at unit 0 falls by the gap; that block 8's wait falls from 2.6 to 0.6 when its load goes ahead of the reloads. That the second loss as a whole goes by the order is shown only in part: with the reloads moved alone the rest is 176.4 and 177.9 in two kernels against 177.7, with unit 0 behind block 8 as well it is 175.1. With both mended the kernel equals before and does not beat it. Of the 3.85 us that products and waits should give, the best version loses 3.4 in the rest (175.1 against 171.7); at block 8 a load's lead is too short still, and whether more raw buffers would give it was not tried.
